# The entry of the first feed-forward product: another order of its seven block products, a sum copied out of its bank early, and later sums of the result

## The chip, the cores and the metric

The kernel runs on one core of a Trainium2 chip. The core has five engines with a queue each: TensorE (PE, matrix products; its weight loads are listed as PEld), VectorE (DVE), ScalarE (ACT), GpSimd (POOL) and SyncE (SP), which here issues most of the DMAs. An engine takes its instructions in the order of its queue; engines wait for each other through semaphores. The metric is the device time of one execution in microseconds (us). The time shown is the median of three executions, and the profile is of a further one.

## The reference

A decoder block on x (1024 tokens, 1024 features): a token mixer (retention and dilated attention), then a feed-forward layer. Only the second half of it matters here:

```python
def rms_norm(x, g):
    xf = x.astype(jnp.float32)
    y = xf * lax.rsqrt(jnp.mean(xf * xf, axis=-1, keepdims=True) + RMS_EPS)
    return (y * g.astype(jnp.float32)).astype(x.dtype)

def squared_relu_mlp(h, w1, w2):
    return jnp.square(jax.nn.relu(h @ w1)) @ w2

# in reference(), after the token mixer
h = modulate(rms_norm(x, norm2_g[l]), sh2, sc2)
x = x + g2[:, None, :] * squared_relu_mlp(h, w_ff1[l], w_ff2[l])
```

`w_ff1` is 1024 x 4096. The change touches the start of `h @ w_ff1` alone.

## The kernel before

**Numbers.** Every float32 product is made of three matmuls on operands that are split into a high part (rounded, type fp32r) and a low part (the rest): low weights with high data, high weights with low data, high with high (`mm3`, lines 201, 203 and 205). So each operand costs an ACT instruction for the high part and a DVE instruction for the low part, and the second can only follow the first.

**Tiling.** Features lie on the 128 partitions, tokens along the free dimension; `G["x1", k]` is feature tile k (0 to 7), 128 x 1024 tokens. `t_(k, half)` is one half of its tokens, 128 x 512. The 4096 output features are made in 16 pairs q of 256 (two tiles of 128 each). For each q the product is a 2 x 2 block product (even and odd input features by first and second token half) in the form with seven products instead of eight. A product is 4 feature tiles m times 3 matmuls of 128 x 512, 12 matmuls, and has a name: "11", "12", "s1", "s3", "s2", "22", "s4" (`ORDER` is the order of a steady pair: 11, s1, s3, s2, 12, 22, s4). `OPERAND` gives the data of each: "11" and "12" use the first token half of the even and of the odd features; "s1" uses t1 (even features, first half minus second half); "s4" uses "22" (odd features, second half); "s3" uses t3 (even minus odd, second half), "s2" uses t2 and "22" uses t4 (sums with further blocks). The data are the same for all 16 pairs and are made once, at the entry; the weights change with q.

**Banks.** A product accumulates in a PSUM bank of 128 x 512 (`BANK`): a of the pair holds 11 and then 11 + 12; d holds s1 and then s1 + s4; b holds s2; c holds s3 and then s3 + 22. There are eight banks, and the first two pairs take all of them. `Blocks.post` takes the banks away: after 11, ACT copies a to u (the pair's first temporary); after s2, DVE computes u = u - b, then v = c - u, then the block "22" of the result, v - d; after 12, ACT makes block "11" from a; after 22, DVE makes block "21" as c - u; after s4, DVE makes block "12" as u + d. `f_out` (lines 2029 to 2048) applies relu and square on ACT to a block, and sends the finished pair to DRAM by SP. Two blocks of one output tile make a tile a, of tag "g0".

**The entry, `ff1` (line 2082).** Pairs 0 and 1 are done together, product by product, while the data are still being made; the row sums of the second token half are only known when the product before has ended. Line 2088 (`norm`) scales the second half of a feature tile. Lines 2104 to 2109 make t1; then 0-s1 and 1-s1 are issued (I write q-n for product n of pair q). Lines 2115 to 2123 make the high parts of operand "22" and both parts of t3; lines 2132 to 2138 the low parts of "22" and both parts of t2, with 0-s3 and 1-s3 issued after the first of them; then 0-s2 and 1-s2, then t4 (`t4`, line 2143) between the two `post(q, "s2")`. `x_split` (2067) does the split: ACT line 2076 or 2079, DVE line 2077 or 2080.

**The loop, `Blocks.run` (line 294).** From there on a list `items` is run: for each product the matmuls; then as many weights prepared as there are free weight slots (`prep`: a DVE sum for s1 to s4, an ACT cast at line 248, a DVE subtraction at 258); then `post`; then `after`, which calls `a_sums`. Product s2 is "ahead": its post comes before the preparation. In the version before, the list is 0-s4, 1-s4, 0-22, 1-22, then all of pair 2, 3 and so on.

**Sums of the result.** The second feed-forward product is also done with seven products, and `a_sums(q, part)` (line 2050) makes its data: two DVE instructions for each part (lines 2055 and 2056, or 2059 and 2060) into a tile of tag "att", and a DMA. The table `late` (2177) says after which product each is made. Part 1 reads the tile of part 0, so that the tile of part 0 is held until then. Tag "att" has eight tiles: four hold t4 for good, and the weights 2-12 and 2-22 and the sums share the other four.

**Loads.** `w1_load(q, part)` (2005) loads half of a pair's raw weights, 512 KB, by SP. In the version before, those of pairs 3 and 4 are issued at the end of the entry (2161 to 2163), before `post(q, "12")`. Their tiles have tag "g0", which they share with the eight `x1` tiles and the result tiles.

Of the kernel before, what the change touches and what calls it, by code (L numbers as in the profile page):

```python
# [11 lines left out]
F32 = mybir.dt.float32  # L12
# [5 lines left out]
P = 128  # L18
# [116 lines left out]
def block_kernel(ctx, tc, io, stop=None, dbg=None):  # L135
    nc = tc.nc
    ctx.enter_context(tc.manual_schedule())

    def fv(t):
        return t.bitcast(F32)  # L140
# [79 lines left out]
    class Blocks:  # L220
# [4 lines left out]
        def __init__(self, name, operands, slots, kept, place, sums, temps, out):  # L225
            self.name, self.x, self.slots, self.kept = name, operands, slots, kept
            self.place, self.sums, self.temps, self.out = place, sums, temps, out
            self.raw, self.w, self.ps, self.t, self.s = {}, {}, {}, {}, {}
            self.low = None

        def prep(self, *items):

# [42 lines left out]
        def post(self, q, n):  # L275

            a, d, b, c = self.ps[q]
            if n == "11":
                self.t[q] = self.temps(f"{self.name}t{q}")
                nc.scalar.copy(self.t[q][0], a)  # L280
                return
            u, v = self.t[q]
            if n == "s2":
                nc.vector.tensor_sub(u, u, b)
                nc.vector.tensor_sub(v, c, u)
                self.out(q, "22", v, d)
            elif n == "12":
                self.out(q, "11", a)
            elif n == "22":
                self.out(q, "21", c, u)  # L290
            elif n == "s4":
                self.out(q, "12", u, d)

        def run(self, items, sums, before=lambda q, n: None, after=lambda q, n: None, ahead=()):

            items_ahead = lambda i: i + 1 < len(items) and items[i + 1][1] in ahead
            for i, (q, n) in enumerate(items):
                before(q, n)  # L300
                self.mm(q, n)
                if n in ahead:
                    self.post(q, n)
                while sums and len(self.slots) > 1:
                    self.prep(sums.pop(0))
                if not items_ahead(i):
                    self.flush()
                if n not in ahead:
                    self.post(q, n)
                after(q, n)  # L310

# [1362 lines left out]
    G = {}  # L1674
# [34 lines left out]
    def mh(name):  # L1709
        return G["mh"].tile([P, 512], F32R, tag="mh", bufs=32, name=name)  # L1710
# [209 lines left out]
    def x1_load(f, src=None):  # L1920

        t = G["p"].tile([P, S], F32, tag="g0", bufs=8, name=f"x1{'r' if src else ''}_{f}")
        nc.sync.dma_start(t, (src or io["xT"])[f])
        G["x1", f] = t
# [80 lines left out]
    def w1_load(q, part):  # L2005

        if q < 2:
            t = G["p"].tile([P, 1024], F32, tag="g1", bufs=8, name=f"w1r{q}{part}")
        elif q < 3:
            t = wraw.tile([P, 1024], F32, tag="raw", name=f"w1r{q}{part}")  # L2010
        else:
            t = G["p"].tile([P, 1024], F32, tag="g0", bufs=8, name=f"w1r{q}{part}")
        nc.sync.dma_start(t, io["w_ff1"][2 * q + part - 1])
        BF.raw[q, part] = t
# [9 lines left out]
        return G["mp"].tile([P, 2, 512], F32, tag="rl", bufs=2, name=name)  # L2024

    def f_temps(name):
        return [G["mp"].tile([P, 512], F32, tag=t, bufs=2, name=name + t) for t in ("nsq", "h2t")]

    def f_out(q, n, x, y=None):

# [19 lines left out]
    def a_sums(q, part):  # L2050
# [7 lines left out]
        else:  # L2058
# [4 lines left out]

    BF = Blocks("f", X, ["g1"] * 4 + ["att*"] * 4 + ["att"] * 2 + ["att*"] * 2 + ["wh", "wl"] * 3,
                lambda kind: kind in ("att", "wh", "wl"), f_place, f_sums, f_temps, f_out)

    def x_split(name, m, src, pool, tag, bufs, k=None):

        if tag == "mh":
            hi, lo = mh(f"x{name}{m}h"), mh(f"x{name}{m}l")  # L2070
        else:
            t = pool.tile([P, 1024], F32R, tag=tag, bufs=bufs, name=f"x{name}{m}")
            hi, lo = t[:, :512], t[:, 512:]
        X[name, m] = hi, lo
        if k is None:
            nc.scalar.copy(hi, src)
            return lambda: nc.vector.tensor_sub(lo, src, fv(hi))
        sh = mods[:, SH2 + k:SH2 + k + 1]
        nc.scalar.activation(hi, src, AF.Identity, bias=sh)
        return lambda: nc.vector.scalar_tensor_tensor(lo, src, sh, fv(hi), op0=ALU.add, op1=ALU.subtract)  # L2080

    def ff1(ahead):
        def t_(k, half):
            return G["x1", k][:, 512 * half:512 * half + 512]

        def norm(k):
            t = t_(k, 1)
            nc.vector.scalar_tensor_tensor(t, t, a2[:, k:k + 1], G["rb"], op0=ALU.mult, op1=ALU.mult)


        BF.mm(0, "11", range(3))
        G["rs"] = rstd_rows(G["acc", "n21"], "n21", G["mp"], lambda: BF.prep((2, "11"), (2, "s1")))
        BF.mm(0, "11", range(3, 4))
        BF.post(0, "11")
        BF.mm(1, "11", range(2))
        G["rb"] = rstd_bcast(G["rs"], 0, 4, "n21")
        BF.mm(1, "11", range(2, 4))
        BF.post(1, "11")
        BF.prep((2, "s3"))
        BF.mm(0, "12")  # L2100
        BF.mm(1, "12")
        low = None
        for m in range(4):
            norm(2 * m)
            t1 = t_(2 * m, 0)
            nc.vector.tensor_sub(t1, t1, t_(2 * m, 1))
            if low:
                low()
            low = x_split("t1", m, t1, None, "mh", 32)
        norm(1)  # L2110
        low()
        BF.mm(0, "s1")
        BF.mm(1, "s1")
        lows = []
        for m in range(4):
            if m > 0:
                norm(2 * m + 1)
            lows.append(x_split("22", m, t_(2 * m + 1, 1), None, "mh", 32, 2 * m + 1))
            t3 = t_(2 * m, 1)
            nc.vector.scalar_tensor_tensor(t3, t3, dsh[:, m:m + 1], t_(2 * m + 1, 1), op0=ALU.add, op1=ALU.subtract)  # L2120
            if m > 0:
                low()
            low = x_split("t3", m, t3, G["p"], "g1", 8)

        def t2(m):
            k = 2 * m + 1
            t = t_(k, 1)
            lows[m]()
            nc.vector.scalar_tensor_tensor(t, t, mods[:, SH2 + k:SH2 + k + 1], t_(2 * m, 0), op0=ALU.add, op1=ALU.add)
            return x_split("t2", m, t, G["p"], "g1", 8)  # L2130

        for m in range(4):
            l = t2(m)
            low()
            low = l
            if m == 0:
                BF.mm(0, "s3")
                BF.mm(1, "s3")
        low()
        BF.mm(0, "s2")  # L2140
        BF.mm(1, "s2")

        def t4(m):
            k = 2 * m + 1
            t = t_(k, 0)
            nc.vector.scalar_tensor_tensor(t, t, mods[:, SH2 + k:SH2 + k + 1], t_(k, 1), op0=ALU.add, op1=ALU.subtract)
            return x_split("t4", m, t, A["r1"], "att", 8)

        low = t4(0)
        BF.post(0, "s2")  # L2150
        low()
        low = t4(1)
        BF.post(1, "s2")
        low()
        low = t4(2)
        l = t4(3)
        low()
        l()
        for k in range(NK):
            del G["x1", k]  # L2160
        for q in (3, 4):
            for part in (1, 2):
                w1_load(q, part)
        for q in range(2):
            BF.post(q, "12")
        sums = [(q, n) for q in range(2, NQ) for n in ORDER]
        items = [(q, n) for n in ("s4", "22") for q in range(2)] + sums

        def before(q, n):
            if q > 2 and n == ORDER[0] and q + 2 < NQ:  # L2170
                for part in (1, 2):
                    w1_load(q + 2, part)
            if q == NQ - 1 and n in ("s2", "12"):
                for f in range(3):
                    x1_load(f + 3 * (n == "12"), x1_d)

        late = {(0, "22"): (0, 0), (1, "22"): (1, 0), (2, "11"): (0, 1), (2, "12"): (1, 1)}
        late.update({(q + 1, n): (q, part) for q in range(2, 4 * NS) for part, n in enumerate(("11", "s1"))})

        def after(q, n):  # L2180
            if (q, n) in late:
                a_sums(*late[q, n])
            if q == NQ - 2 and n in ("12", "22"):
                b_raw(0, "11", int(n == "22"))
            if q == NQ - 1:
                second_ahead(n)

        BF.run(items, sums[3:], before, after, ("s2",))
        x1_load(6, x1_d)
        x1_load(7, x1_d)  # L2190
        b_x(1, 0)
        b_x(1, 1)
# [387 lines left out]
```

## Time and profile before

| | us |
|---|---|
| time, median of 3 runs | 2221.26 (2217.66 to 2222.94) |
| profiled execution, its own time | 2222.6 |
| span of the profiled execution, first to last instruction | 2220.8 |
| granted TensorE clock, mean | 0.995 of full |
| first matmul of 0-11 to first matmul of 3-11 | 1566.60 to 1640.25 |

Times within the span are us from its start. A row of the timeline has start, duration, engine, line, operation, output and inputs, and in brackets the idle time before it and what ended that. A row of the waits has who waited, for whom, us in total, times, the longest. A row of a window has the stretch and its length, the busy time of each engine with its instruction count, the granted clock (PEclk), the share of the DMA engines and GB/s. In the names, `fp` is a bank of this stage, `fw` a weight tile, `xt` and `x22` data, `ft..nsq` the temporary u, `ft..h2t` v, `as` a sum of the result, `w1r` raw weights. Buffer numbers are left out, so t2, t3 and t4 are all "xt". Matmuls are pipelined: at the full clock, one of 128 x 512 is listed with 0.39 us and starts 0.227 us after the one before.

### The profile page before, as it was taken

The page shows a single profiled execution, that of the slowest core. Times are in us where ns is not written, and L with a number is a line of the kernel's source. Part 1 is how long each engine was busy: PE and PEld are TensorE (multiplying, and loading weights), DVE is VectorE, ACT ScalarE, POOL GpSimd, SP SyncE. Part 2 cuts the span into 40 slices and gives each one's busy share as a digit, 9 for nine tenths or more (in the row PEclk, how much of TensorE's full clock was granted, in tenths as well). Part 3 has the DMA queues.
Part 4 walks back from the last instruction along what each step waited for, and adds up shares of the span by engine and source line. Part 5 has one row for each costly group of instructions (what it writes and reads, how often), then busy time and mean ns, then how long its engine had stood idle before and what let it go on. Part 6 is the DMA issues. An engine that isn't in the chain of part 4 may idle for free.

```text
span 2220.8 us, 27106 instructions
## 1 busy us (share of the span) xinstructions
PE 2168.2 (98%) x10082; PEld 1796.1 (81%) x10082; DVE 1469.8 (66%) x2303; ACT 912.6 (41%) x1671; POOL 155.1 (7%) x176
## 2 busy tenths in 40 slices
PE   7999999999999999999999999999999999999998
PEld 4888888878878888888788788888778888788887
DVE  6757777754467877855554653777866665787855
ACT  4432233224334544544534524534444445533412
POOL 0100110000012112200000000001000000000003
PEclk9999999999999999999999999999999999999999
DMA  9869999634675555569523364654234444745322
GB/s 384 219 204 305 276 324 271 191 118 174 240 280 170 190 181 196 179 190 271 159 79 106 103 226 173 238 185 138 79 143 145 150 147 183 253 134 173 121 86 76
DMA packets 157602, 414.15 MB, mean 186 GB/s; under 512 B 27222, under 2 KB 55133, under 8 KB 153054
## 3 DMA queue, kind: packets, MB, share of 16 engines
q1 hardware_dynamic: 149598, 364.19, 46.8%
q0 software_dynamic: 7872, 48.24, 9.4%
q8 instruction: 79, 1.29, 0.2%
q14 instruction: 53, 0.43, 0.1%
HBM read 321.51 MB, written 156.13 MB: 215 GB/s over the span
## 4 chain that ended last, share of the span: by engine, by line
PE 87%; DVE 6%; ACT 3%; issue 1%; DMA 1%; POOL 0%; SPq 0%; POOLq 0%; DVEq 0%; ACTq 0%
PE qap L203 5%; PE qap L201 5%; PE qap L205 5%; PE fp L201 4%; PE fp L203 4%; PE fp L205 4%; PE rg L201 3%; PE rg L203 3%; PE rg L205 3%; PE f2a L203 2%; PE f2a L205 2%; PE f2a L201 2%; PE ak L201 2%; PE ak L203 2%; PE ak L205 2%; PE va L203 1%
## 5 line engine op out<-in xcount | busy, mean ns | idle before, releaser
L201 PE MATMUL qap<-hh,qaw 128*128 128x512 f32 x216 | 84.1, 389 | 0.0
L205 PE MATMUL qap<-hh,qaw 128*128 128x512 f32 x216 | 84.1, 389 | 0.0
L203 PE MATMUL qap<-hl,qaw 128*128 128x512 f32 x216 | 84.0, 389 | 0.0
L625 POOL TENSOR_TENSOR j<-qk,j 128x512 fp32r<-128x512 f32 x32 | 43.3, 1353 | 452.5 <-ACT j L624 452.5
L2039 ACT ACTIVATE a<-a 128x512 f32<-128x512 f32 x48 | 30.3, 632 | 79.2 <-DVE a L2038 79.2
L1936 POOL TENSOR_TENSOR accnf<-accnf,sqnf 128x256 f32<-128x256 f32 (+1 forms) x18 | 16.6, 921 | 620.6 <-ACT sqnf L1935 620.6
L1393 ACT ACTIVATE P<-P,ng 128x128 f32<-128x128 f32 (+1 forms) x96 | 41.9, 438 | 38.9 <-DVE ng L1390 38.9
L258 DVE TENSOR_TENSOR fw<-w1r,fw 128x512 fp32r<-128x512 f32 x48 | 32.9, 688 | 36.2 <-ACT fw L248 36.2
L2225 ACT CAST w2h<-w2s 128x512 fp32r<-128x512 f32 x36 | 22.4, 621 | 78.3 <-DVE w2s L2263 75.7
L201 PE MATMUL fp<-h2h,fw 128*128 128x512 f32 x128 | 50.0, 391 | 0.0
L205 PE MATMUL fp<-h2h,fw 128*128 128x512 f32 x128 | 49.8, 389 | 0.0
L203 PE MATMUL fp<-h2l,fw 128*128 128x512 f32 x128 | 49.8, 389 | 0.0
L203 PE MATMUL roa<-rl,rwh 128*128 128x512 f32 x128 | 49.8, 389 | 0.0
L205 PE MATMUL roa<-rh,rwh 128*128 128x512 f32 x128 | 49.8, 389 | 0.0
L201 PE MATMUL roa<-rh,rwl 128*128 128x512 f32 x128 | 49.8, 389 | 0.0
L1774 DVE TENSOR_TENSOR rwl<-rwl,rwh 128x1024 fp32r<-128x1024 f32 x25 | 30.2, 1220 | 29.1 <-ACT rwh L1804 29.1
L1936 POOL TENSOR_TENSOR accn<-accn,sqn 128x512 f32<-128x512 f32 x12 | 15.5, 1294 | 481.0 <-ACT sqn L1935 481.0
L645 ACT COPY sm<-sT 128x128 f32<-128x128 f32 x32 | 8.5, 265 | 98.7 <-PE sT L638 98.7
L201 PEld LDWEIGHTS qap<-hh,qaw 128*128 128x128 f32 x216 | 40.5, 188 | 8.5
L205 PEld LDWEIGHTS qap<-hh,qaw 128*128 128x128 f32 x216 | 40.5, 188 | 8.4
L203 PEld LDWEIGHTS qap<-hl,qaw 128*128 128x128 f32 x216 | 40.6, 188 | 8.4
L258 DVE TENSOR_TENSOR qaw<-wa,qaw 128x512 fp32r<-128x512 f32 x54 | 36.9, 686 | 12.1 <-ACT qaw L248 12.1
(3063 smaller groups left out, 7187.2 us busy)
## 6 DMA issues: line engine op xcount, KB each, us to landing
v<-vd SPq DMA_DIRECT2D x32, 512.0 KB, 4.8
raw<-in_w_ada_dram SPq DMA_DIRECT2D x32, 512.0 KB, 5.6
w1r<-in_w_ff_dram SPq DMA_DIRECT2D x32, 512.0 KB, 5.0
vd<-vo SPq DMA_DIRECT2D x24, 512.0 KB, 4.5
yt<-y POOLq DMA_DIRECT2D x6, 2048.0 KB, 16.0
xsd<-as SPq DMA_DIRECT2D x24, 512.0 KB, 2.7
w2r<-in_w_ff2s_dram SPq DMA_DIRECT2D x24, 512.0 KB, 7.0
em<-in_w_ada_dram SPq DMA_DIRECT2D x16, 512.0 KB, 10.2
```

Source lines behind the costliest of these rows:

```text
L201: nc.tensor.matmul(o, wl, xh, start=first, stop=False, skip_group_check=skip)
L203: nc.tensor.matmul(o, wh, xl, start=False, stop=False, skip_group_check=skip)
L205: nc.tensor.matmul(o, wh, xh, start=False, stop=last, skip_group_check=skip)
L258: nc.vector.tensor_sub(t[:, 512:], src, fv(t[:, :512]))
L625: nc.gpsimd.tensor_sub(t[:, 1], src, fv(t[:, 0]))
L645: nc.scalar.copy(sm, ps[:, :C])
L1393: nc.scalar.activation(v, v, AF.Exp, bias=ng[:, blk:blk + 1], accum_out=st[:, g, blk, 2 + a:3 + a])
L1774: nc.vector.tensor_sub(lo, fv(lo), fv(hi))
L1936: (nc.vector if f == 7 else nc.gpsimd).tensor_add(G["acc", key], G["acc", key], sq)
L2039: nc.scalar.activation(o, o, AF.Relu)
L2225: nc.scalar.copy(hi, src)
```

## The change

- In the entry, operand "22" is finished, low parts too, right after t1, and 0-s4 and 1-s4 are the products that follow s1. They add to bank d, which holds s1's sum; so a new `post(q, "s1")` has ACT copy bank d to v first, between the casts of operand "22". Then t3 with 0-s3 and 1-s3, then t2 with 0-s2 and 1-s2, then t4.
- For pairs 0 and 1 `post(q, "s2")` takes v from that copy: u = u - b, v = v + u, block "22" = c - v. It is again three DVE instructions.
- `post(q, "12")` and `post(q, "s4")` of the first two pairs are done in the entry, between the steps of t4.
- The run's list begins with 2-11 and 2-s1, then 0-22 and 1-22, then the rest of pair 2.
- Pair 2 takes its u and v from another tag ("nacc").
- The loads of pair 3 stand behind the finished pairs' posts, those of pair 4 ahead of product 2-22.
- Of the sums, `a_sums(0, 1)` is made after 2-s2 and no longer after 2-11; `a_sums(1, 1)` stays after 2-12.

```diff
@@ Blocks.post
             u, v = self.t[q]
-            if n == "s2":
+            if n == "s1":
+                nc.scalar.copy(v, d)
+                self.held.add(q)
+            elif n == "s2" and q in self.held:
+                nc.vector.tensor_sub(u, u, b)
+                nc.vector.tensor_add(v, v, u)
+                self.out(q, "22", c, v)
+            elif n == "s2":
                 nc.vector.tensor_sub(u, u, b)
                 nc.vector.tensor_sub(v, c, u)
                 self.out(q, "22", v, d)
@@ Blocks.run
-                if n not in ahead:
+                if n not in ahead and n != "s1":
                     self.post(q, n)
@@ f_temps
-        return [G["mp"].tile([P, 512], F32, tag=t, bufs=2, name=name + t) for t in ("nsq", "h2t")]
+        tags = ("nacc", "nacc") if name == "ft2" else ("nsq", "h2t")
+        return [G["mp"].tile([P, 512], F32, tag=t, bufs=2, name=name + t) for t in tags]
@@ ff1
         BF.mm(0, "s1")
         BF.mm(1, "s1")
-        lows = []
         for m in range(4):
             if m > 0:
                 norm(2 * m + 1)
-            lows.append(x_split("22", m, t_(2 * m + 1, 1), None, "mh", 32, 2 * m + 1))
+                low()
+            low = x_split("22", m, t_(2 * m + 1, 1), None, "mh", 32, 2 * m + 1)
+            if m % 2 == 0:
+                BF.post(m // 2, "s1")
+        for m in range(4):
             t3 = t_(2 * m, 1)
             nc.vector.scalar_tensor_tensor(t3, t3, dsh[:, m:m + 1], t_(2 * m + 1, 1), op0=ALU.add, op1=ALU.subtract)
-            if m > 0:
-                low()
+            low()
+            if m == 0:
+                BF.mm(0, "s4")
+                BF.mm(1, "s4")
             low = x_split("t3", m, t3, G["p"], "g1", 8)
-
-        def t2(m):
+        for m in range(4):
             k = 2 * m + 1
             t = t_(k, 1)
-            lows[m]()
             nc.vector.scalar_tensor_tensor(t, t, mods[:, SH2 + k:SH2 + k + 1], t_(2 * m, 0), op0=ALU.add, op1=ALU.add)
-            return x_split("t2", m, t, G["p"], "g1", 8)
-
-        for m in range(4):
-            l = t2(m)
             low()
-            low = l
             if m == 0:
                 BF.mm(0, "s3")
                 BF.mm(1, "s3")
-        low()
-        BF.mm(0, "s2")
-        BF.mm(1, "s2")
+            low = x_split("t2", m, t, G["p"], "g1", 8)
...
-        low = t4(0)
+        l = t4(0)
+        low()
+        BF.mm(0, "s2")
+        BF.mm(1, "s2")
         BF.post(0, "s2")
+        l()
+        low = t4(1)
+        l = t4(2)
         low()
-        low = t4(1)
+        BF.post(0, "12")
         BF.post(1, "s2")
+        l()
+        low = t4(3)
+        BF.post(0, "s4")
         low()
-        low = t4(2)
-        l = t4(3)
-        low()
-        l()
+        BF.post(1, "12")
+        BF.post(1, "s4")
         for k in range(NK):
             del G["x1", k]
-        for q in (3, 4):
-            for part in (1, 2):
-                w1_load(q, part)
-        for q in range(2):
-            BF.post(q, "12")
+        for part in (1, 2):
+            w1_load(3, part)
         sums = [(q, n) for q in range(2, NQ) for n in ORDER]
-        items = [(q, n) for n in ("s4", "22") for q in range(2)] + sums
+        items = sums[:2] + [(0, "22"), (1, "22")] + sums[2:]

         def before(q, n):
+            if (q, n) == (2, "22"):
+                for part in (1, 2):
+                    w1_load(4, part)
             if q > 2 and n == ORDER[0] and q + 2 < NQ:
...
-        late = {(0, "22"): (0, 0), (1, "22"): (1, 0), (2, "11"): (0, 1), (2, "12"): (1, 1)}
+        late = {(0, "22"): (0, 0), (1, "22"): (1, 0), (2, "s2"): (0, 1), (2, "12"): (1, 1)}
```

More of the change, by code (lines that the diff above doesn't have):

```diff
@@ L228, in __init__ @@
             self.raw, self.w, self.ps, self.t, self.s = {}, {}, {}, {}, {}
-            self.low = None
+            self.low, self.held = None, set()
         def prep(self, *items):
```

## The prediction

> **What bounds the kernel now.** I read the page first, then TensorE's waits and the windows of the stage that the change touches, then its timeline, engine by engine.
>
> ```profile
> span 2220.8 us, 27106 instructions
> PE 2168.2 (98%) x10082; PEld 1796.1 (81%) x10082; DVE 1469.8 (66%) x2303; ACT 912.6 (41%) x1671; POOL 155.1 (7%) x176
> ```
>
> TensorE sets the time, so an entry is worth only what it takes away of TensorE's standing still. The waits between 1564 and 1660, and windows by product:
>
> ```profile
> PE fp L201 <- DVE ft2h2t L285: 5.3, 1, 5.3
> PE fp L203 <- DVE xt L2077: 3.6, 4, 1.1
> DVE as L2059 <- PE fp L205: 3.7, 1, 3.7
> 1586.00:1594.90 8.90, 6.36 (x26) 4.30 (x25) 8.72 (x14) 3.92 (x6) 0.00 (x0) 1.00 0.01 2
> 1594.90:1601.90 7.00, 5.93 (x25) 4.27 (x24) 6.59 (x11) 2.15 (x4) 0.00 (x0) 1.00 0.48 150
> 1626.90:1640.20 13.30, 8.01 (x25) 6.38 (x25) 10.66 (x17) 6.84 (x12) 0.00 (x0) 0.74 0.21 80
> 1640.20:1659.20 19.00, 19.00 (x85) 15.73 (x85) 12.61 (x20) 7.87 (x15) 0.00 (x0) 1.00 0.41 152
> ```
>
> In s3 and s2 of pairs 0 and 1 DVE is full (8.72 of 8.90 us) and TensorE waits for it; from 1626.9 TensorE stands for another reason, and at a lower clock; pair 3 runs without a gap, 84 matmuls in 19.04 us. TensorE's timeline at the first matmul of s1, s3, s2, s4, 22, 2-11, around 2-22, and 3-11:
>
> ```profile
> 1580.33 0.39 PE L201 MATMUL fp<-xt10h,fw0s 128*128 128x512 f32 x1
> 1586.07 0.39 PE L201 MATMUL fp<-xt,fw0s 128*128 128x512 f32 x1
> 1594.93 0.39 PE L201 MATMUL fp<-xt,fw0s 128*128 128x512 f32 x1
> 1601.95 0.39 PE L201 MATMUL fp<-x220h,fw0s 128*128 128x512 f32 x1
> 1607.73 0.39 PE L201 MATMUL fp<-xt,fw 128*128 128x512 f32 x1
> 1613.17 0.39 PE L201 MATMUL fp<-h2h,fw 128*128 128x512 f32 x1
> 1626.55 0.39 PE L205 MATMUL fp<-h2h,fw 128*128 128x512 f32 x1
> 1632.22 0.80 PE L201 MATMUL fp<-xt,fw 128*128 128x512 f32 x1 [5.29 <-DVE ft2h2t L285]
> 1632.82 0.63 PE L203 MATMUL fp<-xt,fw 128*128 128x512 f32 x1
> 1637.49 0.39 PE L201 MATMUL fp<-x220h,fw2s 128*128 128x512 f32 x1
> 1640.25 0.39 PE L201 MATMUL fp<-h2h,fw 128*128 128x512 f32 x1
> ```
>
> Without a stall 24 matmuls take 24 x 0.2267 = 5.44 us. So s1 loses 5.74 - 5.44 = 0.30, s3 8.86 - 5.44 = 3.42, s2 7.02 - 5.44 = 1.58, s4 5.78 - 5.44 = 0.34, 22 nothing. 2-22 should start at 1626.78; it starts 5.44 late, and its 12 matmuls take 5.27 in place of 2.72, for they run at half the clock: 2.55 more. Together 13.6 us lie in this entry. That is all the change can win.
>
> **Why 2-22 waits.** Bank c is free for it when DVE has made v of pair 2 (line 285), and DVE was blocked before:
>
> ```profile
> 1622.58 0.69 DVE L258 TENSOR_TENSOR fw<-w1r,fw 128x512 fp32r<-128x512 f32 x1 [0.55 <-ACT fw L248]
> 1626.97 0.69 DVE L2059 TENSOR_TENSOR as<-a,a 128x512 f32<-128x512 f32 x1 [3.70 <-PE fp L205]
> 1630.76 0.68 DVE L284 TENSOR_TENSOR ft2nsq<-ft2nsq,fp 128x512 f32<-128x512 f32 x1
> 1631.48 0.69 DVE L285 TENSOR_TENSOR ft2h2t<-fp,ft2nsq 128x512 f32<-128x512 f32 x1
> ```
>
> The late sum (line 2059) begins when the last matmul of 2-12 ends, 1626.55 + 0.39. Its output has tag "att": four of the eight tiles hold t4, two the weights 2-12 and 2-22, two the sums of part 0. So it takes the tile of weight 2-12 when that product is over, and the post of 2-s2, whose matmuls had ended before, stands behind it in DVE's queue.
>
> **Prices.**
>
> ```profile
> 1591.47 0.74 DVE L2080 SCALAR_TENSOR_TENSOR x221l<-x,mods,x221h 128x512 fp32r<-128x512 f32 x1
> 1592.25 0.75 DVE L2129 SCALAR_TENSOR_TENSOR x<-x,mods,x 128x512 f32<-128x512 f32 x1
> 1592.92 0.69 DVE L2077 TENSOR_TENSOR xt<-x,xt 128x512 fp32r<-128x512 f32 x1
> 1593.52 0.75 DVE L2080 SCALAR_TENSOR_TENSOR x222l<-x,mods,x222h 128x512 fp32r<-128x512 f32 x1
> 1581.36 0.74 DVE L2088 SCALAR_TENSOR_TENSOR x<-x,a,n21rb 128x512 f32<-128x512 f32 x1
> 1582.13 0.72 ACT L2079 ACTIVATE x220h<-x,mods 128x512 fp32r<-128x512 f32 x1 [0.64 <-DVE x L2088]
> 1575.12 0.59 ACT L280 COPY ft1nsq<-fp 128x512 f32<-128x512 f32 x1 [3.46 <-PE fp L205]
> 1608.72 0.58 ACT L2036 ACTIVATE a<-fp 128x512 f32<-128x512 f32 x1
> 1609.87 0.60 ACT L248 CAST fw2s<-fs 128x512 fp32r<-128x512 f32 x1
> 1610.38 0.62 ACT L248 CAST fw<-w1r 128x512 fp32r<-128x512 f32 x1
> ```
>
> DVE, start to start: 0.60 behind a two-operand instruction, 0.67 behind a three-operand one, 0.03 more than the full duration (0.72 and 0.78) where it reads the result before it. ACT: a cast takes 0.62 and the next starts 0.51 later; a relu with its square 1.15. From one engine to the next 0.03 to 0.06 us. I laid both queues end to end with these. For the old order that gives 1632.22 for 2-22, as the trace has; so the method holds for what it has been told.
>
> **The change part by part.**
>
> *The operands.* What matters is when the low part of a product's fourth data tile is ready: its eleventh matmul needs it, 10 x 0.2267 = 2.27 us after the first. No DVE instruction is added. From `norm` of tile 1 at 1581.36 DVE's queue up to the low part of the fourth "22" tile is ten instructions (three low parts and three `norm` in turns, t1's low part and the first t3 among them): nine steps of 0.60 or 0.67 and 0.15 of waiting make 6.2 us, so it starts at 1587.54 and ends at 1588.29. Needed at 1586.07 + 2.27 = 1588.34, so 0-s4 runs through, with nothing to spare. From there t3 and t2 each take four pairs of 0.60 + 0.67: t3's fourth low part is ready at 1593.4, needed at 1591.6 + 2.3 = 1593.9; t2's at 1598.5, needed at 1597.1 + 2.3 = 1599.4. The old queue had the four low parts of "22" in front of t2 and behind t3, and interleaved t3 with "22"; that is where 3.42 and 1.58 went. t4's last low part: 1609.5, needed at 1608.1 + 2.3 = 1610.4. So s4, s3, s2 and 22 lose about 0.1 in all: **5.2 us won** (3.42 + 1.58 + 0.34 - 0.1).
>
> *The copies of s1's banks.* Two ACT instructions are added, 0.59 us each by the ACT row of line 280. The first waits for 0-s1's last matmul (1583.5) with the casts of "22" behind it; that is the 0.15 of waiting above. In the old queue ACT has 3.92 us of work in the 8.90 of s3, so they hide, but without the DVE work around them they would cost 0.6 each.
>
> *Posts moved forward.* 2-11 and 2-s1 need banks b and a of pair 0. The DVE subtraction frees b at 1600.7, 2-11 starts at 1602.5; ACT's relu of 0-12 frees a at 1605.2, just as 2-s1 is to start (1605.3). No loss, 0.1 at most.
>
> *The loads of pair 3.* In the old order they went out early:
>
> ```profile
> 1595.12 0.33 SPq L2013 DMA_DIRECT2D w1r<-in_w_ff_dram  x1
> DMA to landing us min/median/max: 3.4/5.0/6.2
> ```
>
> Now SP has two DMAs of finished pairs ahead of them, the second behind the square of 1-s4. ACT's queue before it: block "22" of pair 1 is given at 1606.8 by DVE; four pairs of relu and square and one cast, 4 x 1.15 + 0.6 = 5.2 and the rest of the last, until 1612.4. So the first load goes out at 1612.85. The loads of this kind (second row: all 32) take 3.4 to 6.2 us to land. This one is the first of two and has 256 KB ahead of it; I take 4.0, and 3.4 to 6.2 as bounds. Weight 3-11 is then there at 1616.85, and its cast, which is now prepared with 0-22, waits 0.8 us for it. DVE's queue is behind that cast. *What is late next:* cast 0.62, low part at 1617.5, then block "21" of pair 0, two sums, the weight sum of 3-s1 (0.60 + 0.60 + 0.72 + 0.67), end of that at 1620.8; cast of 3-s1 until 1621.5; its low part, block "21" of pair 1, two sums, the weight sum of 3-s3, u and then v of pair 2 (0.60 + 0.60 + 0.72 + 0.67 + 0.60 + 0.72) end at **1626.1**. TensorE, with 2.72 us a product, has ended 2-12 at 1621.7. So 2-22 still waits, 4.5 us for the same line 285, and starts at 1626.2.
>
> *The late sums.* `a_sums(0, 1)` is now behind 2-s2's post and finds 2-12 over: the 3.70 us block is gone. But DVE now has both pairs' "21" blocks and four sums between 2-s1 and 2-s2, and that fills the place. Weights of pair 4: loaded at 1633, wanted by their cast at 1638; at 4 us no wait.
>
> *The half clock.* After 5.29 us of standing 12 matmuls ran at half the clock; gaps of 1.1 us in s3 left them at 0.39 us. A shorter gap did it too:
>
> ```profile
> 658.25 0.79 PE L201 MATMUL kv<-v,kl 128*128 128x512 f32 x1 [2.52 <-DVE kl L655]
> 658.84 0.63 PE L203 MATMUL kv<-v,kh 128*128 128x512 f32 x1
> ```
>
> So the 4.5 us gap also brings it. A cost of 0.8 us (a short stretch, mostly within the gap) to 2.55 (as before); I take the middle, 1.65. [...]
>
> **The sum.** 2-22 starts at 1626.2, 2-s4 2.83 and 3-11 2.72 later, at 1631.75, where the trace has 1640.25: 8.5 us earlier. Of that goes the half clock, 1.65; a wait of 0.76 in 3-22 that the fuller DVE queue would cause lies inside it. Left: **6.85 us**. The profiled execution took 2222.6, so 2215.75; it stands 1.3 above the median shown, which makes 2214.4 for the median, 0.31% less. Everything behind pair 3 keeps its order.
>
> **The rivals.** *The late sums were all of it*: with that block gone 2-22 doesn't wait at all. 5.2 + 5.44 + 2.55 = 13.2 won, 2208.1. For it: line 2059 stood for 3.70 of the 5.29 us. Against: DVE's queue above, which is as long without it. *Loads late and the half clock at its longest*: landing after 6.2 us moves 2-22 by 2.2, and 8.5 - 2.2 - 2.55 leaves 3.75 (a wait of 1.8 in 3-22, for pair 4's loads are late too, lies inside the half clock): 2217.5. *Slower*: the same load is the place. Each us of landing beyond 6 costs one at 2-22 and one at 3-22; at 8.4 us the win is used up, at 10 us the kernel is 3 us slower, 2224.4. For it: SP now issues it 17.7 us later than the row at 1595.12, into the stretch where results are stored. Against: no load of these landed after more than 6.2. *The copies don't hide*: if the first holds the casts of "22" a step longer, 0-s4 waits 0.6; 2215.0, within the forecast.
>
> **How the numbers follow.** Forecast as worked out (5 to 8.5 won): 0.62. Late sums all of it: 0.10. Late loads and longest half clock: 0.17. Slower: 0.11. From landing 3.4 to 6.2 and the half clock 0.8 to 2.55 the forecast reaches from 2213 to 2217.5; with the first rival's side and a run-to-run spread of some 2 us I give 2210 to 2220. A change under 0.2% (4.4 us) can't be told from none; so faster 0.73 (the forecast nearly whole, the first rival), same 0.16, slower 0.11.
>
> **What would show it.** Right: in the waits, no entry of TensorE for line 2077 over 0.2 us; 0-s4 at 1586.1 by the same clock, 0-s3 at 1591.6, 0-s2 at 1597.1, 2-11 at 1602.5; one wait of 2-22 for line 285, 3.9 to 6.7 us, with 0.63 us matmuls behind it; a cast of 3-11 that waits for a DMA; line 2059 with no wait for PE. Wrong: 2-22 without a wait; casts of "22" so late that 0-s4 stands; a wait of 3-22 over 1 us; or PE gaps in 22, which would tell of t4.

## The result, and the profile after

The median of the changed kernel is 2213.55 us (2209.44 to 2214.90, 6 runs) beside 2221.27 us (2217.66 to 2222.94, 6 runs) of the kernel before on the same chip: 7.72 us less, ratio 0.9967, 95% interval 0.9957 to 0.9977. On a second chip it was 2211.22 us beside 2220.84 us, 0.9965 (0.9953 to 0.9977). The forecast was 2214.4 us.

The profiled execution took 2212.59 us, its span is 2210.8 us. First the head of the page, then TensorE's longest wait in the entry (us in total, times, longest), then TensorE's timeline (start, duration; in brackets the idle time before and who ended it) at the first matmuls of 0-11, 0-s4, 0-s3, 0-s2, 2-11, around 2-22, and of 3-11 and 4-11:

```profile
span 2210.8 us, 27102 instructions
PE 2165.6 (98%) x10082; PEld 1796.1 (81%) x10082; DVE 1469.3 (66%) x2303; ACT 913.8 (41%) x1673; POOL 155.2 (7%) x176
```

```profile
PE fp L201 <- DVE ft2nacc L292: 3.3, 1, 3.3
```

```profile
1564.20 0.39 PE L201 MATMUL fp<-h2h,fw 128*128 128x512 f32 x1
...
1583.70 0.39 PE L201 MATMUL fp<-x220h,fw0s 128*128 128x512 f32 x1
...
1589.25 0.39 PE L201 MATMUL fp<-xt,fw0s 128*128 128x512 f32 x1
...
1594.69 0.39 PE L201 MATMUL fp<-xt,fw0s 128*128 128x512 f32 x1
...
1600.13 0.39 PE L201 MATMUL fp<-h2h,fw 128*128 128x512 f32 x1
...
1619.20 0.39 PE L205 MATMUL fp<-h2h,fw 128*128 128x512 f32 x1
1622.87 0.80 PE L201 MATMUL fp<-xt,fw 128*128 128x512 f32 x1 [3.28 <-DVE ft2nacc L292]
1623.46 0.63 PE L203 MATMUL fp<-xt,fw 128*128 128x512 f32 x1
...
1631.04 0.39 PE L201 MATMUL fp<-h2h,fw 128*128 128x512 f32 x1
...
1650.08 0.39 PE L201 MATMUL fp<-h2h,fw 128*128 128x512 f32 x1
```

For comparison, 0-11 and 4-11 in the kernel before:

```profile
1566.60 0.39 PE L201 MATMUL fp<-h2h,fw 128*128 128x512 f32 x1
...
1659.29 0.39 PE L201 MATMUL fp<-h2h,fw 128*128 128x512 f32 x1
```

The entry starts 2.40 us earlier (1566.60 - 1564.20), where nothing was changed; so places in the entry are compared by their distance from the first matmul of 0-11, or with 2.40 added. From there to 4-11 it is 92.69 us before (1659.29 - 1566.60) and 85.88 us after (1650.08 - 1564.20): **6.81 us are won inside the entry**. Of the 10.0 us between the two profiled executions the rest is 2.4 ahead of it and 0.8 behind it. The waits for line 2077 (now 2085) are gone: s4, s3 and s2 follow each other in 5.44 or 5.55 us, 24 matmuls without a stall being 5.44. One wait is left, of 2-22 for DVE's second sum of pair 2 (line 285, now 292), 3.28 us in place of 5.29, and behind it matmuls of 0.63 us again. The late sum that stood for 3.70 us starts at 1626.01 without one.

What was ahead of the post, on ACT, SP and DVE of the changed kernel (cast of 3-11 behind another cast; the instruction of ACT's queue that waits for the load of 3-11, with its duration in ns and its start; issue of the first load of pair 3; the sums u and v; the late sum):

```profile
1613.04 0.62 ACT L248 CAST fw2s<-fs 128x512 fp32r<-128x512 f32 x1 [1.04 <-DVE fs L243]
1613.65 0.62 ACT L248 CAST fw<-w1r 128x512 fp32r<-128x512 f32 x1
L248 ACTq EVENT_SEMAPHORE  x1: 17/17/17, 1613.6 to 1613.6; - x1
```

```profile
1609.21 0.38 SPq L2020 DMA_DIRECT2D w1r<-in_w_ff_dram  x1
```

```profile
1621.41 0.68 DVE L291 TENSOR_TENSOR ft2nacc<-ft2nacc,fp 128x512 f32<-128x512 f32 x1
1622.12 0.69 DVE L292 TENSOR_TENSOR ft2nacc<-fp,ft2nacc 128x512 f32<-128x512 f32 x1
...
1626.01 0.69 DVE L2067 TENSOR_TENSOR as<-a,a 128x512 f32<-128x512 f32 x1
```

The cast of 3-11 hardly waits for its DMA: the load goes out at 1609.21, ACT's wait for it is over at 1613.6, some 4.4 us later, and the cast starts at 1613.65, right behind the one before it. So the load came just in time, with nothing to spare.

### The profile page after: what moved, and what is told of

Its sections match the earlier page's. It is cut to its first block, busy times and chain, and to the rows that moved or that the text cites. A ratio compares the mean times of both kernels' runs of the same rounds, so it can differ in the third digit from the quotient of the medians.

```text
span 2210.8 us, 27102 instructions
## 1 busy us (share of the span) xinstructions
PE 2165.6 (98%) x10082; PEld 1796.1 (81%) x10082; DVE 1469.3 (66%) x2303; ACT 913.8 (41%) x1673; POOL 155.2 (7%) x176
## 4 chain that ended last, share of the span: by engine, by line
PE 88%; DVE 6%; ACT 3%; issue 1%; DMA 1%; POOL 0%; POOLq 0%; SPq 0%; DVEq 0%; ACTq 0%
PE qap L201 5%; PE qap L203 5%; PE qap L205 5%; PE fp L201 4%; PE fp L203 4%; PE fp L205 4%; PE rg L201 3%; PE rg L203 3%; PE rg L205 3%; PE f2a L203 2%; PE f2a L201 2%; PE f2a L205 2%; PE ak L201 2%; PE ak L203 2%; PE ak L205 2%; PE va L203 1%
```

## The experiments

The medians of the kernel before differ from chip to chip by up to 2.8 us (2218.51 to 2221.27), and executions of one kernel on one chip by 5 us (2209.44 to 2214.90 above), so two readings are given of each: the ratio to the kernel before on the same chip, and the trace, in us from the first matmul of 0-11 to that of 4-11.

| kernel | wait of 2-22 | half clock in the entry | to 4-11 | ratio (95% interval) |
|---|---|---|---|---|
| before | 5.29 | 6.83 | 92.69 | 1 |
| changed | 3.28 | 6.83 | 85.88 | 0.9967 (0.9957 to 0.9977) |
| changed, second execution | 3.38 | none | 83.96 | 0.9965 (0.9953 to 0.9977) |
| late sums alone | none | none | 85.67 | 0.9968 (0.9957 to 0.9980) |
| product order alone | 5.29 | 6.83 and 3.41 | 93.07 | 1.0007 (0.9998 to 1.0017) |
| list as before | none | 3.41 | 85.98 | 0.9974 (0.9964 to 0.9985) |
| gap filled | 0.58 | none | 83.85 | 0.9966 (0.9954 to 0.9978) |
| loads later | 5.09 | 3.41 | 86.65 | 0.9975 (0.9964 to 0.9986) |
| s1 copied twice | 3.31 | none | 84.53 | 0.9965 (0.9952 to 0.9979) |
| sums spread, one ahead per pair | 1.97 | none | 81.93 | 0.9949 (0.9937 to 0.9961) |
| sums spread, none ahead | 1.19 | none | 83.49 | 0.9960 (0.9948 to 0.9972) |
| the same, gap filled | none | none | 83.34 | 0.9955 (0.9943 to 0.9967) |
| sums on POOL | 6.62 | 6.83 | 88.78 | 0.9983 (0.9975 to 0.9992) |

"Half clock" is the length of the stretch, within the entry, in which the trace's granted clock is 0.50. It is in one execution of a kernel and not in the next (see "The changed kernel once more"), so differences of some 2 us between two single traces can be owed to it alone (85.88 beside 83.96 us for the changed kernel).

**The late sums alone.** The kernel before with

```
-        late = {(0, "22"): (0, 0), (1, "22"): (1, 0), (2, "11"): (0, 1), (2, "12"): (1, 1)}
+        late = {(0, "22"): (0, 0), (1, "22"): (1, 0), (2, "s2"): (0, 1), (2, "12"): (1, 1)}
```

and the loads of pair 4 ahead of 2-22.

> The kernel before, with one part of the change alone: the second sums of pair 0 are given behind 2-s2 and not behind 2-11 (and the loads of pair 4, whose buffers these sums free, are asked for ahead of 2-22). The product order, the posts and the list are those of before. Theory (DVE queue laid end to end): the stalls of s3 and s2 stay (some 5 us), but 2-22 waits only 0.3 us in place of 5.29, so its matmuls run at full clock; 3-22 then waits 0.7; 4-11 starts 85.9 us after the first matmul of 0-11 (92.69 before, 85.88 in the changed kernel). So this part alone gives 6.8 us: about 2214.4, the same as the whole change. Rival (the prediction's accounting, that the block moves but the place is filled by the other sums, and that the product order brings 5.2 of the 8.5 us): 2-22 still waits 3 us or more with 0.63 us matmuls, 4-11 at 89 or later, 2218 or more.

TensorE's wait in s3 and s2, its first matmul of 0-11, and the end of DVE's queue ahead of 2-22:

```profile
PE fp L203 <- DVE xt L2077: 3.7, 4, 1.1
```

```profile
1565.14 0.39 PE L201 MATMUL fp<-h2h,fw 128*128 128x512 f32 x1
```

```profile
1624.11 0.68 DVE L284 TENSOR_TENSOR ft2nsq<-ft2nsq,fp 128x512 f32<-128x512 f32 x1
1624.83 0.69 DVE L285 TENSOR_TENSOR ft2h2t<-fp,ft2nsq 128x512 f32<-128x512 f32 x1
```

Measured 85.67 for the 85.9 expected: 7.0 us of the 92.69 come from one line and the loads that have to follow it, with the stalls of s3 and s2 (the four of line 2077) all in place. 2-22 runs through, for TensorE comes to it just as late as DVE has v; so the 5.29 us of its wait and the half clock behind them are gone.

**The product order alone.** The changed kernel with the posts, loads, list and `late` of before:

```
-        items = sums[:2] + [(0, "22"), (1, "22")] + sums[2:]
+        items = [(0, "22"), (1, "22")] + sums
...
-        late = {(0, "22"): (0, 0), (1, "22"): (1, 0), (2, "s2"): (0, 1), (2, "12"): (1, 1)}
+        late = {(0, "22"): (0, 0), (1, "22"): (1, 0), (2, "11"): (0, 1), (2, "12"): (1, 1)}
```

> The changed kernel with only its product order left: s4 second on a copied bank, operands made in the order of their use. The posts, the early loads of pairs 3 and 4, the list (0-22, 1-22, then pair 2) and the place of the second sums are as before. Theory (one part's gain turns into the other's wait): s4, s3 and s2 run without a wait as in the changed kernel, 5.2 us won, but 0-22 now follows 1-s2 at once and waits for its t4 tiles, 0.1 to 1.7 us at a time and 3.6 us in all, and 2-22 waits 5.3 us as before with the half clock behind it. 4-11 at 91.7 us after the first matmul of 0-11 (92.69 before), 1.0 us won, about 2220.3, which is no measurable difference. Rival (the product order is worth its 5.2 us by itself): 4-11 at 87.5, 2216.

TensorE's timeline in 0-22 and at 2-22:

```profile
1601.25 0.51 PE L201 MATMUL fp<-xt,fw 128*128 128x512 f32 x1 [0.58 <-ACT xt L2084]
1603.24 0.67 PE L203 MATMUL fp<-xt,fw 128*128 128x512 f32 x1 [1.49 <-DVE xt L2085]
...
1630.66 0.77 PE L201 MATMUL fp<-xt,fw 128*128 128x512 f32 x1 [5.29 <-DVE ft2nacc L292]
```

93.07, no gain at all, and none in the medians either (1.0007, 0.9998 to 1.0017). The direction was as expected: what s3 and s2 no longer wait, 0-22 waits for t4, and 2-22 then waits its 5.29 us as ever. The 1.4 us beyond the expected 91.7 go with a half clock that was not in the sum: it begins in 0-22, behind the pieces of waiting there (a matmul of 0.67 us at 1603.24 already).

**The list as before.** The changed kernel with only `items = [(0, "22"), (1, "22")] + sums`.

> The changed kernel with one part undone: 2-11 and 2-s1 stand again behind 0-22 and 1-22. Theory: 0-22 then waits for its t4 tiles, 4.2 us in all, in pieces of at most 1.7 us, and 2-22 does not wait at all, since the DVE work ahead of it has the time of two products more; no long gap, so the full clock everywhere: 4-11 at 84.8 us after the first matmul of 0-11 (85.88 in the changed kernel), about 2212.5, a us under the changed kernel. Rival (pieces of 1 to 2 us also halve the clock): 0-22 with 0.63 us matmuls, 4-11 at 87.3, 2215. Second rival (moving the two products is what won the time): 2-22 waits more than 3.3 us, 4-11 beyond 88.

```profile
1603.17 0.50 PE L203 MATMUL fp<-xt,fw 128*128 128x512 f32 x1 [1.67 <-DVE xt L2085]
...
1605.27 0.79 PE L203 MATMUL fp<-xt,fw 128*128 128x512 f32 x1 [0.23 <-DVE xt L2085]
```

85.98, between the 84.8 with full clock and the 87.3 of the rival. 2-22 does not wait, as the theory had it; 0-22 does, in pieces of up to 1.67 us, and a stretch of 3.41 us at half clock follows. So moving 2-11 and 2-s1 ahead is a trade: it takes the waits out of 0-22 and puts one in front of 2-22.

**The gap filled.** In the changed kernel, ahead of 2-22, with the first data tile of "11" as both operands (`w0`, `x0`) and the bank of 3-11 as the output (`nxt[0]`):

```
+                for i in range(12):
+                    nc.tensor.matmul(nxt[0], w0[:, :P], x0, start=i == 0, stop=i == 11, skip_group_check=True)
```

> The changed kernel, with twelve matmuls more between 2-12 and 2-22 whose result nobody uses (0.2267 us each at full clock, 2.72 us, into the bank that 3-11 overwrites): they keep TensorE at work for most of the 3.28 us in which it stands there. Theory (the half clock behind the gap costs some 2.6 us): 2-22 still waits for the second sum of pair 2 and starts at the same time, but its matmuls take 0.39 us; 3-11 starts 2.6 us earlier, 64.2 us after the first matmul of 0-11 in place of 66.84; 3-22 then waits some 0.6 us that the slow product hid; 4-11 starts at 83.9 in place of 85.88, and the time is 2.0 us under that of the changed kernel, about 2211.5. Rival (the slow product costs nothing, because DVE's queue sets the time of 3-11 or 3-22 anyway): 3-22 waits for what is won, 4-11 at 85.9 and 2213.5 as now. Second rival (the clock is halved by something else than standing): 2-22 still with 0.63 us matmuls, 3-11 at 66.8 or later.

```profile
1617.22 2.88 PE L270 MATMUL fp<-h2h 128*128 128x512 f32 x12
1620.69 0.50 PE L201 MATMUL fp<-xt,fw 128*128 128x512 f32 x1 [0.58 <-DVE ft2nacc L298]
```

3-11 came at 64.20 and 4-11 at 83.85; 64.2 and 83.9 were expected. With the clock full, the slow product costs nothing and 3-22 shows the wait of 0.3 that it hid. The median does not resolve it (0.9966, as the changed kernel), and the next run tells why.

**The changed kernel once more.**

> The changed kernel once more, as the base for the three runs beside it. 2-22 waits 3.3 us for the second sum of pair 2, its matmuls take 0.63 us; 3-11 at 66.8 us and 4-11 at 85.9 us after the first matmul of 0-11; ratio to the kernel before 0.9967.

The wait was 3.38 us, and the clock stayed full: 4-11 at 83.96. The granted clock about the gap (stretch, length, busy us with count of PE, PEld, DVE, ACT and POOL; then the granted clock, DMA share and GB/s); first the execution of the result, then this one:

```profile
1621.65:1625.07 3.42, 2.20 (x5) 1.81 (x6) 3.02 (x5) 2.02 (x4) 0.00 (x0) 0.50 0.83 307
1625.07:1628.48 3.41, 3.41 (x9) 2.64 (x9) 2.58 (x5) 2.56 (x5) 0.00 (x0) 0.50 0.08 31
```

```profile
1615.00:1640.00 25.00, 21.62 (x96) 17.54 (x95) 19.62 (x32) 13.51 (x23) 0.00 (x0) 1.00 0.62 224
```

About a gap of nearly the same length (3.28 and 3.38 us) the clock is 0.50 for 6.83 us in the first and 1.00 throughout in the second; what makes the difference was not shown. So the cost of the half clock behind 2-22 is 2.6 us in one execution of the same kernel (8.17 us from 2-22 to 3-11 beside 5.61) and nothing in another.

**The loads later.** One DMA more ahead of the loads of pair 3, so that they stand where the prediction took them to stand:

```
+        nc.sync.dma_start(dram.tile([P, 512], F32, name="late"), M["out", 1][0][:, 512:])
         for part in (1, 2):
             w1_load(3, part)
```

> The changed kernel with one DMA more in SP's queue ahead of the loads of pair 3: it stores block 12 of pair 1 and so waits for the square behind 1-s4, which is where the prediction took the loads to stand (in the changed kernel they wait only for the square behind 1-12, and go out 1.25 us earlier). Theory (that step is what put the wait of 2-22 at 4.5 us, and the prediction's chain behind the load is right): the cast of 3-11 waits 0.5 to 1.3 us for its DMA, and 2-22 waits 3.9 to 4.6 us in place of 3.3. Rival (the load is not on the path): no cast waits and 2-22 waits 3.3 us.

SP's issues, the cast of 3-11, and 2-22:

```profile
1607.92 0.32 SPq L2172 DMA_DIRECT2D late<-a  x1
1608.33 0.87 SPq L2020 DMA_DIRECT2D w1r<-in_w_ff_dram  x2
```

```profile
1613.36 0.62 ACT L248 CAST fw<-w1r 128x512 fp32r<-128x512 f32 x1 [1.76 <-DMA w1r<-in_w_ff_dram]
```

```profile
1622.57 0.70 PE L201 MATMUL fp<-xt,fw 128*128 128x512 f32 x1 [5.09 <-DVE ft2nacc L292]
```

The cast waits 1.76 us and 2-22 waits 1.81 more than in the changed kernel (5.09 - 3.28): the whole lateness of the load arrives at 2-22. Both are a half us beyond what was expected, because the load took 5.0 us to its cast (1613.36 - 1608.33) and not the 4.0 of the prediction or the 4.4 of the changed kernel.

**s1 copied twice.** `nc.scalar.copy(v, d)` stands twice in `post`.

> The changed kernel with each copy of an s1 bank made twice (two ACT instructions of 0.59 us more). Theory (the prediction: the casts of 22 have nothing to spare behind the first copy): 0-s4 waits 0.6 us in its last data tile, and what follows is 0.6 us later to the end of the entry, 2-22's wait being no shorter because DVE's chain moves with it: 4-11 at 84.6 us without a half clock and 86.5 with one (83.96 and 85.88 in the changed kernel's two traces). Rival (the copies lie beside other work): no wait in 0-s4. Second rival (0-s4 waits but 2-22's wait takes it up): 4-11 as in the changed kernel.

```profile
1583.50 0.50 PE L201 MATMUL fp<-x223h,fw0s 128*128 128x512 f32 x1
1584.29 0.50 PE L203 MATMUL fp<-x223l,fw0s 128*128 128x512 f32 x1 [0.28 <-DVE x223l L2089]
...
1621.20 0.50 PE L201 MATMUL fp<-xt,fw 128*128 128x512 f32 x1 [3.31 <-DVE ft2nacc L293]
```

The matmul at 1584.29 starts 0.79 us after the one before, and not 0.227: 0.56 are lost, of which the view calls 0.28 idle because the first of the two is listed with 0.50. 4-11 at 84.53 for the 84.6 expected, 0.57 later than the execution with full clock, and the wait of 2-22 is hardly shorter (3.31 beside 3.38). So the single copies are hidden with nothing to spare, and what is lost early in the entry is lost to the end. The ratio (0.9965) does not show so little.

**The sums spread.** In the changed kernel

```
+        late = {(0, "22"): (0, 0), (2, "s2"): (1, 0), (2, "12"): (0, 1), (2, "22"): (1, 1)}
+        late.update({(q + 1, n): (q, part) for q in range(2, 4 * NS) for part, n in enumerate(("s2", "12"))})
```

> The changed kernel with its sums spread: for pairs 0 and 1 one sum each behind 0-22, 2-s2, 2-12 and 2-22 (so only one sum, and not two, stands ahead of pair 2's own in DVE's queue), and for the later pairs behind s2 and 12 of the next pair and not behind 11 and s1. Theory (DVE's queue ahead of 2-22 sets its start, 1.4 us a sum): the wait of 2-22 falls by 1.4 to 1.9 us, and 3-22, which had the sums of pair 2 ahead of it, does not wait. 3-11 at 63.0 and 4-11 at 82.0 us if the shorter wait leaves the clock alone (3.9 us under the changed kernel), 65.6 and 84.6 if it is still halved (1.3 us under it). Rival (not DVE's queue but the post's own inputs, 2-s2 and the copy, set 2-22): wait as now, 4-11 at 85.9.

```profile
1621.94 0.50 PE L201 MATMUL fp<-xt,fw 128*128 128x512 f32 x1 [1.97 <-DVE ft2nacc L292]
```

4-11 at 81.93 (82.0 expected), full clock, 2208.68 us in the median where the changed kernel has 2211.22 on that chip. It is the best of the kernels run, and beats the changed kernel by 2 us in the trace (83.96, full clock too) and 2.5 in the medians; the two intervals still overlap.

With none of the four sums ahead of pair 2's post (`(2, "s2"): (0, 0), (2, "12"): (1, 0), (2, "22"): (0, 1), (2, "s4"): (1, 1)`, and pair 4's loads ahead of 2-s4):

> As the run before, but no sum at all ahead of pair 2's own: the four stand behind 2-s2, 2-12, 2-22 and 2-s4, and the loads of pair 4, whose buffers the third frees, go ahead of 2-s4. Theory: 2-22 waits 1.5 us in place of 3.3 and 3-22 not at all; 3-11 at 62.2 and 4-11 at 81.2 at full clock, 4.7 us under the changed kernel (2208.8 where that has 2213.5); with the clock halved 64.8 and 83.8. Rival (pair 4's loads, now asked for 2.8 us later, are late): 4-11 itself waits, for a cast of its weights, 2 us or more.

```profile
1636.07 0.62 ACT L248 CAST fw<-w1r 128x512 fp32r<-128x512 f32 x1 [3.28 <-DMA w1r<-in_w_ff_dram]
1636.60 0.58 ACT L280 COPY ft3nsq<-fp 128x512 f32<-128x512 f32 x1
```

```profile
1637.23 0.50 PE L201 MATMUL fp<-h2h,fw 128*128 128x512 f32 x1 [0.62 <-ACT ft3nsq L280]
...
1641.37 0.50 PE L201 MATMUL fp<-xt,fw 128*128 128x512 f32 x1 [1.09 <-DVE ft3h2t L292]
```

3-11 came at 62.08, as expected (62.2), but 4-11 at 83.49 and not 81.2. The rival's mechanism is there, in another place: pair 4's loads are late, its cast stands 3.28 us in ACT's queue, and the copy of 3-11's bank stands behind the cast; so 3-12 waits for ACT and 3-22 for DVE. With six unused matmuls in the gap it is the same:

> As the run before, with six matmuls more whose result nobody uses ahead of 2-22 (1.36 us at full clock), so that TensorE does not stand at that place. Theory: whatever the clock did in the run before, here no matmul takes 0.63 us; 3-11 at 62.2 and 4-11 at 81.2, 4.7 us under the changed kernel. Rival (the six get in the way of 2-22, or the clock is halved by something else): later than the run before.

83.34: there was no half clock to take away, and the late cast is still there.

**The sums on POOL.** In `a_sums` three instructions on POOL in place of two on DVE, for part 0:

```
+            nc.gpsimd.tensor_sub(r[:, 0], e[:, :512], e[:, 512:])
+            nc.gpsimd.tensor_sub(r[:, 1], e[:, 512:], e[:, :512])
+            nc.gpsimd.tensor_sub(r[:, 1], r[:, 1], o[:, 512:])
```

> The changed kernel with the sums for the second product worked out by POOL, which is idle in this stage, in three two-operand instructions each (1.35 us each by the trace's POOL rows of 128x512) in place of two on DVE. Theory (DVE's queue ahead of 2-22 is the bound, and the sums are the part of it that nobody near waits for): 2-22 waits 1.2 to 1.5 us as in the run without sums ahead, 3-12 and 3-22 do not wait, since the buffers for pair 4's loads are free earlier than there; no matmul at half clock; 3-11 at 62.1 and 4-11 at 81.2 us, ratio to the kernel before 0.9945. Rival (POOL and DVE hold each other up): DVE's instructions beside POOL's take longer than 0.69 us, 2-22 waits 2.5 us or more.

POOL's and DVE's timelines in the same stretch:

```profile
1608.66 1.78 POOL L2063 TENSOR_TENSOR as<-a 128x512 f32<-128x512 f32 x1 [37.71 <-ACT a L2048]
...
1623.61 1.59 POOL L2070 TENSOR_TENSOR as<-as,a 128x512 f32<-128x512 f32 x1
```

```profile
1608.60 0.68 DVE L243 TENSOR_TENSOR fs<-fs,w1r 128x512 f32<-128x512 f32 x1
1609.21 1.78 DVE L258 TENSOR_TENSOR fw2s<-fs,fw2s 128x512 fp32r<-128x512 f32 x1
...
1624.00 0.68 DVE L2046 TENSOR_TENSOR a<-fp,ft1nsq 128x512 f32<-128x512 f32 x1
```

The rival holds: beside POOL, DVE's 0.69 us instructions take up to 1.78 us and 2-22 waits 6.62 us. 4-11 comes 2.9 us later than in that execution of the changed kernel which has the half clock too (88.78 beside 85.88), and 4.8 us later than in the one without. The DVE instruction at 1624.00 (line 2046), one input of which is a bank (`fp`), took 0.68 us beside POOL's at 1623.61.

## Why the prediction was right, and where it was not

The time came out by the mechanism that was forecast: the waits for operands gone, one wait of 2-22 for the same sum left, a half clock behind it. With 2.40 added, 0-s4, 0-s3, 0-s2 and 2-11 stand at 1586.10, 1591.65, 1597.09 and 1602.53 where 1586.1, 1591.6, 1597.1 and 1602.5 were forecast; 3-11 at 1633.44, where 1631.75 and 1.65 make 1633.40. Two of the signs named beforehand did not come: a cast of 3-11 that waits for its DMA, and a wait of 2-22 of 3.9 to 6.7 us (it was 3.28). The agreement of that last number, 3-11, is luck, for two errors cancel:

- **The loads of pair 3 were placed one DMA too late.** The prediction put SP's second store behind the square of 1-s4 and the first load at 1612.85. That store sends block 11 only and waits for the square of 1-12, so the load went out at 1609.21 + 2.40 = 1611.61, 1.24 earlier; it took 4.4 us and not 4.0, landed just as its cast was due, and the 0.8 us wait of the cast did not occur. The term "2-22 waits 4.5 us" measured 3.28, and 2-22 started at 1625.27 and not 1626.2, 0.9 earlier. The chain behind the load was right, as the run with later loads shows (1.76 us of lateness, 1.81 us at 2-22); its 4.0 us for the landing was too short in both (4.4 and 5.0).
- **The half clock was taken at 1.65 us, the middle between two bounds.** The lower one, 0.8, was the author's estimate, and no run shows it. In the profiled execution it cost 8.17 us from 2-22 to 3-11 (1631.04 - 1622.87) beside 5.61 in the second execution, 2.6 us, the upper bound; in that second execution it cost nothing, which is below the lower one. In the run with the loads later, where the stretch is 3.41 us and not 6.83, the same way takes 7.19 (1629.76 - 1622.57), 1.6 more than at full clock: there the middle is met. So what it costs differed between two executions of one kernel, and the middle is no forecast for a single one.

The copies were hidden with nothing to spare, as said (0.56 us lost in 0-s4 once they are doubled). A wait of 3-22 was forecast to lie inside the half clock, and does: none in the result, 0.3 us where the clock stayed full.

What the prediction had wrong without paying for it is **how the gain divides**. It booked 5.2 us to the operands, and held that the late sum's block moves but that DVE's other sums fill its place. As a sum over the whole change this holds. But the product order by itself is worth nothing (93.07 beside 92.69) and the moved late sums by themselves 7.0 us, because DVE's u and v of pair 2 set when 2-22 can start. With the late sums alone v ends 60.38 us after the first matmul of 0-11 (1624.83 + 0.69 - 1565.14, the last number being that execution's first matmul of 0-11), in the changed kernel 58.61 (1622.12 + 0.69 - 1564.20): TensorE's 5.2 us bring DVE forward by 1.8 only, and the other 3.4 are about what 2-22 now waits (3.28). So the rival "the late sums were all of it" is wrong in its number (13.2 us, no wait of 2-22) and right in its sense: that part alone wins as much as the whole change did in the execution with the half clock, and 1.7 us less than in the one without (85.67 beside 85.88 and 83.96). The rival by which the kernel gets slower, loads of pair 3 that land 2 us or more beyond any seen, was not tried further than the 1.76 us above.

## What to carry to other kernels

Taking stalls out of an engine wins only as much as the engine that it waits for next moves forward with it; lay that other queue end to end up to the next common point before booking the gain. Of two edits made together, try each alone: here one brings all and the other nothing, and the second pays only when work with a distant due time (the sums for a later product) is also moved behind the near one, and no further, since the buffers that it holds delay the next loads (the cast of pair 4's weights waited 3.28 us with no sum ahead). (Sums spread in the old product order were not run; but in the trace with the late sums alone they could take away no more than the wait of 3-22, 0.33 us of its 85.67, while the new order with spread sums has 81.93.) A store that shares a queue with a load is placed by the block that it sends, so read its operand and not only its place in the program.

## What the hardware did that was not expected

The granted clock of TensorE differed between two executions of one kernel about nearly the same gap. In the changed kernel it was 0.50 for 6.83 us (1621.65 to 1628.48) with a wait of 2-22 of 3.28 us, and 1.00 from 1615 to 1640 in the second execution, with a wait of 3.38 us; with s1 copied twice it was full too, with a wait of 3.31 us. In the run with the list as before it was 0.50 from 1605.27 to 1608.68, where 0-22 had waited in pieces of 1.67 us at most. What decides it was not shown. In the run with the gap filled the clock was full; whether the twelve matmuls kept it so, or it would have been full without them as in the second execution of the changed kernel, was not shown either.

The traces differ in this way elsewhere too: ahead of the kernel's end that of the kernel before has 0.50 in three stretches, from 657.83, 1128.87 and 1630.63 us on, and the first of the changed kernel in two, from 495.26 and 1621.65 on. In the two traces of the changed kernel the half clock goes with 1.92 us up to 4-11 (85.88 - 83.96), beside 5 us between the executions of one kernel on one chip; this is part of why medians did not resolve what the traces do.

The other surprise was DVE beside POOL: 0.69 us became up to 1.78, so that work moved to an idle POOL came back as a loss, of 2.9 us beside the execution with the same half clock.
